# A PEER encoder kernel: VectorE's work beside each unit in a new order, two gate buffers, nine weight buffers

## The chip, the cores and the metric

The kernel runs on one core of a Trainium2 chip. The metric is the device time of one execution, in microseconds. A core has TensorE (matmuls, PE in the profile, with PEld for its weight loads), VectorE (DVE), ScalarE (ACT), GpSimd (POOL) and SyncE (SP), each with a queue of its own that is worked off in order; SyncE, ScalarE and GpSimd also issue DMA transfers.

## What is computed

One encoder layer on 512 tokens of width 2048, all in float32: an input projection, attention and a recurrence side by side, an output projection, and then PEER, a mixer that picks for each token and each of 8 heads the best 16 of 16,384 single-neuron experts. The change lies in the PEER part:

```python
def peer(x, w_pq, sub_k1, sub_k2, u_emb, v_emb):
    q = (xt @ w_pq).reshape(T, PEER_HEADS, 2, PEER_HALF)
    s1 = jnp.einsum('thd,hkd->thk', q[:, :, 0], sub_k1, preferred_element_type=jnp.float32)
    s2 = jnp.einsum('thd,hkd->thk', q[:, :, 1], sub_k2, preferred_element_type=jnp.float32)
    ...
    sc, sel = lax.top_k(cand, PEER_TOPK)
    eidx = jnp.take_along_axis(cidx, sel, axis=-1)
    gates = jax.nn.softmax(sc, axis=-1)
    ...
        uc = u_emb[ic]
        act = jax.nn.gelu(jnp.einsum('cd,ced->ce', xc, uc))
        vc = v_emb[ic]
        return jnp.einsum('ce,ced->cd', (gc * act).astype(vc.dtype), vc)
```

## The kernel before

**Two ways to the same sum.** For the first 160 tokens the chosen rows of `u_emb` and `v_emb` are gathered: 160 row steps with U and 160 with V, each one indirect DMA of GpSimd (128 rows of 2048) into one of three `gat` buffers and one VectorE instruction over it (`gu` L1159, `gv` L1181). The generator `gather_gen` does one such step whenever it is advanced. For the other 352 tokens PEER is computed densely: all 16,384 experts, in 128 blocks of 128, with a matrix of gates that is zero for experts not chosen.

**Units.** The dense part is a chain of 256 units of TensorE with 48 matmuls each. A U block (`u_block`) multiplies a block of U with the 352 tokens and gives `ga`, its gelu. A V unit (`v_unit`) multiplies one of eight chunks of V with eight weighed blocks and adds to `acc` (`v_evict`, two VectorE additions). Every matmul is done three times on values that are split in a high and a low part, so each unit first needs its operand split: a 1 MB load `raw` (SyncE, two buffers), `hi`, a cast on ScalarE (L280), and `lo`, a subtraction on VectorE (L292), two buffers each. `take` at the start of a unit issues the split of the next unit. The low part of a unit is needed by its second or third matmul.

**Stages of the dense part.** The number of U blocks ahead of the first V unit is `lead0`, 31. The first 28 of them carry hooks, four in each block, one after every fourth of its matmuls. `stage_plan` fills the hooks with what is left of the routing (`pair`, `sc`, `pick`, softmax) and then with 88 steps (`g`) that build the gate matrix: VectorE makes two one-hots of 128x512 for a group of four tokens (L1219), ScalarE multiplies one of them by the gates in four instructions (L1222), four TensorE matmuls give the gates, ScalarE copies them out (`stg`, L1227), and after every eight steps a store puts 2 MB in DRAM (`gd`). The plan also sets the steps of the gather (`tick`). It counts costs for TensorE, VectorE and ScalarE and adds a task when VectorE and ScalarE stand no later than TensorE. The first 14 hooked blocks are called routing below, the other 14 the one-hot stage.

Then come 16 passes of eight V units each; between two passes stand the U blocks that are still missing: three in each of the first four passes (short passes), up to eight later (long passes). Before a pass, its eight blocks must be weighed (`weigh`): VectorE multiplies `ga` by the gates in `G` (L1333), ScalarE casts the product (`Wh`, L1336), VectorE subtracts (`Wl`, L1337). `G` holds four blocks, has one buffer and is loaded anew by SyncE after the fourth of them is weighed. There are ten buffers of `Wh` and `Wl` (PR + LEAD). A block whose weighing comes long after its U block is stored to DRAM and reloaded into `gr` (two buffers); these are 38.

**What sets the order.** The order on each engine is that of the program text; no scheduler changes it. In a V unit VectorE gets: lo of the next unit, the eviction of this unit, in two units of a pass a weighing, then the due row steps (1.3 a unit). In a U block: lo of the next, the due row steps, then the weighings that `W_AT` (long passes) or a rule of three per block (short passes) puts there.

## Time and profile before

| | |
|---|---|
| three runs | 3173.66, 3175.65, 3178.24 us, median 3175.65 |
| the profiled execution | 3176.04 us; span 3174.2 |
| mean granted clock of TensorE | 0.972 |
| busy: PE, DVE, ACT, POOL | 93%, 71%, 38%, 26% of the span |
| the dense part | from 878.9 us to the end |

The span reaches from the first to the last instruction; the time has some 2 us around it. A granted clock of 1.00 is TensorE's full 2.4 GHz, and the other level is 1.2 GHz. Busy shares are means over stages that differ, so the table of stages below is read first, and then the waits of each stage: who stood still, and what ended it.

### The profile page before, as it was taken

The page shows a single profiled execution, that of the slowest core. Times are in us where ns is not written, and L with a number is a line of the kernel's source. Part 1 is how long each engine was busy: PE and PEld are TensorE (multiplying, and loading weights), DVE is VectorE, ACT ScalarE, POOL GpSimd, SP SyncE. Part 2 cuts the span into 40 slices and gives each one's busy share as a digit, 9 for nine tenths or more (in the row PEclk, how much of TensorE's full clock was granted, in tenths as well). Part 3 has the DMA queues.
Part 4 walks back from the last instruction along what each step waited for, and adds up shares of the span by engine and source line. Part 5 has one row for each costly group of instructions (what it writes and reads, how often), then busy time and mean ns, then how long its engine had stood idle before and what let it go on. Part 6 is the DMA issues. An engine that isn't in the chain of part 4 may idle for free. (4 is left out here: it accounts for less than half of the span.)

```text
span 3174.2 us, 41739 instructions
## 1 busy us (share of the span) xinstructions
PE 2967.4 (93%) x16965; PEld 2751.6 (87%) x16965; DVE 2251.3 (71%) x3099; ACT 1199.9 (38%) x1705; POOL 823.8 (26%) x539
## 2 busy tenths in 40 slices
PE   8999999999997888689888999999999999999998
PEld 6777766788887888689788999999999999999997
DVE  5763466447975888457767787877777778777875
ACT  5652344334443777232222233233232232232323
POOL 0000211023532113123322323332323323323321
PEclk9999999999998999889899999999999999999999
DMA  5212311242235778778777889889888899898883
GB/s 219 86 69 97 127 47 40 80 160 83 80 136 205 276 285 302 256 275 314 257 288 279 320 312 336 319 318 334 319 322 335 311 335 331 308 337 323 314 307 141
DMA packets 155728, 760.64 MB, mean 240 GB/s; under 512 B 13200, under 2 KB 68000, under 8 KB 69584
## 3 DMA queue, kind: packets, MB, share of 16 engines
q1 hardware_dynamic: 99264, 375.38, 32.8%
q0 software_dynamic: 48000, 345.73, 29.0%
q10 hardware_dynamic: 8272, 36.87, 3.0%
q8 instruction: 133, 2.18, 0.3%
q14 instruction: 59, 0.48, 0.0%
HBM read 719.36 MB, written 38.57 MB: 239 GB/s over the span
## 5 line engine op out<-in xcount | busy, mean ns | idle before, releaser
L292 DVE TENSOR_TENSOR lo<-raw,hi 128x2048 fp32r<-128x2048 f32 x307 | 707.9, 2307 | 404.7 <-ACT hi L280 400.9
L280 ACT CAST hi<-raw 128x2048 fp32r<-128x2048 f32 x316 | 602.2, 1906 | 632.7 <-PE ps_v L1370 276.8
L308 PE MATMUL ps_u<-H,hi 128*128 128x352 f32 x2048 | 674.2, 329 | 37.2 <-ACT hi L280 37.2
L310 PE MATMUL ps_u<-H,lo 128*128 128x352 f32 x2048 | 671.6, 328 | 29.9 <-DVE lo L292 29.7
L1369 PE MATMUL ps_v<-Wh,hi 128*128 128x352 f32 x2048 | 663.4, 324 | 33.1 <-ACT hi L280 27.2
L1371 PE MATMUL ps_v<-Wh,lo 128*128 128x352 f32 x2048 | 667.4, 326 | 16.2 <-DVE lo L292 16.2
L309 PE MATMUL ps_u<-L,hi 128*128 128x352 f32 x2048 | 668.9, 327 | 0.0
L1370 PE MATMUL ps_v<-Wl,hi 128*128 128x352 f32 x2048 | 665.1, 325 | 0.5
L1173 POOL DMA_INDIRECT gv<-in_v_emb_dram,idx x160 | 305.0, 1906 | 735.5 <-DVE gu L1159 550.2
L1157 POOL DMA_INDIRECT gu<-in_u_emb_dram,idx x160 | 299.7, 1873 | 737.4 <-DVE x L1181 542.2
L308 PEld LDWEIGHTS ps_u<-H,hi 128*128 128x128 f32 x2048 | 392.4, 192 | 39.1 <-ACT hi L280 38.9
L310 PEld LDWEIGHTS ps_u<-H,lo 128*128 128x128 f32 x2048 | 391.6, 191 | 36.5 <-DVE lo L292 36.5
L1369 PEld LDWEIGHTS ps_v<-Wh,hi 128*128 128x128 f32 x2048 | 388.3, 190 | 37.6 <-ACT hi L280 30.3
L1371 PEld LDWEIGHTS ps_v<-Wh,lo 128*128 128x128 f32 x2048 | 388.1, 190 | 21.8 <-DVE lo L292 21.7
L309 PEld LDWEIGHTS ps_u<-L,hi 128*128 128x128 f32 x2048 | 392.2, 192 | 0.0
L1370 PEld LDWEIGHTS ps_v<-Wl,hi 128*128 128x128 f32 x2048 | 387.6, 189 | 2.0 <-DVE Wl L1337 2.0
L1159 DVE SCALAR_TENSOR_TENSOR gu<-gu,xng 128x2048 f32<-128x2048 f32 x160 | 365.1, 2284 | 19.3 <-DMA gu<-in_u_emb_dram,idx 19.3
L1181 DVE SCALAR_TENSOR_TENSOR x<-gv,w,x 128x2048 f32<-128x2048 f32 x128 | 300.2, 2345 | 0.1
L1381 DVE TENSOR_TENSOR acc<-ps_v,acc 128x352 f32<-128x352 f32 x240 | 123.8, 521 | 160.1 <-PE ps_v L1371 159.3
L1131 ACT ACTIVATE ga<-ps_u 128x352 f32<-128x352 f32 x128 | 59.0, 461 | 385.9 <-PE ps_u L310 385.9
L1222 ACT ACTIVATE ohA<-ohA,lt 128x128 f32<-128x128 f32 x352 | 112.6, 392 | 56.6 <-DVE ohA L1219 53.7
L1336 ACT CAST Wh<-ga 128x352 fp32r<-128x352 f32 x90 | 43.7, 485 | 237.4 <-DVE ga L1333 237.4
(310 smaller groups left out, 3781.9 us busy)
## 6 DMA issues: line engine op xcount, KB each, us to landing
raw<-in_u_t_dram SPq DMA_DIRECT2D x128, 1024.0 KB
raw<-in_v_t_dram SPq DMA_DIRECT2D x128, 1024.0 KB
raw<-in_w_dram SPq DMA_DIRECT2D x28, 1024.0 KB
gd<-stg ACTq DMA_DIRECT2D x11, 2048.0 KB
G<-gd SPq DMA_DIRECT2D x32, 704.0 KB
raw<-in_w_out_dram SPq DMA_DIRECT2D x16, 1024.0 KB
raw<-in_w_pq_dram SPq DMA_DIRECT2D x16, 1024.0 KB
ad<-ga ACTq DMA_DIRECT2D x38, 176.0 KB
```

What stands on the lines that cost most here:

```text
L280: A.copy(hi, raw)
L292: en.tensor_tensor(lo[:, c], raw[:, c], hi.bitcast(F32)[:, c], op=ALU.subtract)
L308: T.matmul(ps, ah, bh, start=first, stop=False)
L309: T.matmul(ps, ah, bl, start=False, stop=False)
L310: T.matmul(ps, al, bh, start=False, stop=last)
L1157: P.indirect_dma_start(out=g, out_offset=None, in_=u_emb, in_offset=bass.IndirectOffsetOnAxis(ap=ix, axis=0))
L1159: V.scalar_tensor_tensor(out=g, in0=g, scalar=1.0, in1=xs_t["x"], op0=ALU.mult, op1=ALU.mult, accum_out=a_t[h][:, k:k + 1])
L1173: P.indirect_dma_start(out=g, out_offset=None, in_=v_emb, in_offset=bass.IndirectOffsetOnAxis(ap=ix, axis=0))
L1181: V.scalar_tensor_tensor(out=d, in0=g, scalar=wk, in1=d, op0=ALU.mult, op1=ALU.add)
L1369: T.matmul(ps[:, 0:TD], hi[:, cc], Wh, start=j == 0, stop=False)
L1370: T.matmul(ps[:, 0:TD], hi[:, cc], Wl, start=False, stop=False)
L1371: T.matmul(ps[:, 0:TD], lo[:, cc], Wh, start=False, stop=j == PR - 1)
```

## The change

*Planner.* `LEAD` falls from 2 to 1, so there are nine weight buffers. The costs of the planner's tasks are raised, VectorE starts with 4 us on its account, and an engine that is early is credited with 2 us instead of 4. `lead0` becomes 40: 37 U blocks carry hooks, with the same 88 gating steps (one to three in a hook) and 33 row steps, and 55 blocks are stored and reloaded instead of 38. There are six short passes with three U blocks (two in the weighing order 3, 2, 2), one with seven, and then eight and seven. In the long passes one block is weighed beside each U block.

*Gating.* For steps with even number VectorE multiplies the one-hot by the gates in one instruction of 128x512, in place of ScalarE's four.

*Gather.* The rows are issued two steps ahead of the step that uses them, and a task `prime` issues the first two some time before the first step.

*Beside a unit.* A new function, `beside`, is called at the start of each unit after `take`: at most one due row step, then lo of the next unit, then the eviction of the V unit before (it was done in that unit itself), then the weighings, and then a second row step if it is due. `flush_lo` is also called ahead of each hook.

*Buffers.* `G` has two buffers and is loaded two groups ahead; `gr` has three, `ua` three instead of four. The scratch `jk` moves to PSUM.

*Last pass.* The pieces of the final output follow V units 5, 6 and 7 instead of 4, 5 and 6, and the last block is weighed after the last U block.

```diff
-LEAD = 2
+LEAD = 1
-W_AT = ((), (0,), (1,), (), (2, 3), (4,), (5,), ())
...
-        dve, act = max(dve, pe - 4), max(act, pe - 4)
+        dve, act = max(dve, pe - 2), max(act, pe - 2)
...
         for i in range(r):
...
+            ready = [b for b in todo if b < done + i]
+            now = ready[:-(-len(todo) // (r - i))]
+            todo = todo[len(now):]
             run.append(now)
+            order += [("w", b) for b in now] + [("u", done + i)]
...
-        elif b < seen[-1] - 3:
+        elif b < seen[-1] - 1:
             spilled.add(b)
...
-    uap, _ = pool("ua", bufs=4, side="right")
+    uap, _ = pool("ua", bufs=3, side="right")
...
         load_x(0)
...
+        tiles = [issue(*f) for f in seq[:2]]
+        yield
+        for n, (kind, h, k) in enumerate(seq):
+            if n + 2 < len(seq):
+                tiles.append(issue(*seq[n + 2]))
+            (u_step if kind == "u" else v_step)(tiles.pop(0), h, k)
...
-        for t in range(NB):
-            A.activation(out=Ao[:, t, :], in_=Ao[:, t, :], func=AF.Copy, scale=lt[:, 2, ta + t:ta + t + 1])
+        if n % 2:
+            for t in range(NB):
+                A.activation(out=Ao[:, t, :], in_=Ao[:, t, :], func=AF.Copy, scale=lt[:, 2, ta + t:ta + t + 1])
+        else:
+            V.tensor_tensor(Ao, Ao, lt[:, 2, ta:ta + NB].unsqueeze(2).to_broadcast([128, NB, 128]), op=ALU.mult)
...
-    gp, _ = pool("G", bufs=1)
-    sml, _ = pool("sml", bufs=2)
-    grp, _ = pool("gr", bufs=2)
+    gp, _ = pool("G", bufs=2)
+    grp, _ = pool("gr", bufs=3)
...
-            load_g(b // GRP + 1)
+            load_g(b // GRP + 2)
...
-    def tick():
-        due["now"] += due["per"]
+    late_ev = []
+
+    def beside(ws=(), gather=True):
+
+        if gather:
+            due["now"] += due["per"]
+        if due["now"] >= 1.0:
+            due["now"] -= 1.0
+            next(gg, None)
+        flush_lo()
+        while late_ev:
+            v_evict(*late_ev.pop(0))
+        for b in ws:
+            weigh(b)
         while due["now"] >= 1.0:
             due["now"] -= 1.0
             next(gg, None)
...
-                jk = sml.tile([128, 512], F32, tag="jk", name="jk", bufs=1)
+                jk = psB.tile([128, 512], F32, tag="B", name="jk")
...
-            pss = v_unit(g, c)
-            v_evict(g, c, pss)
+            pss = v_unit(g, c, (b0,) if c == 1 and 0 < g < NP - 1 else (), g < NP - 1)
+            late_ev.append((g, c, pss))
...
-                if c in (4, 5, 6):
-                    final(c - 4)
+                if c in (5, 6, 7):
+                    final(c - 5)
...
         for ws in runs[g]:
-            u_block(ub)
+            u_block(ub, beside=lambda: beside(ws))
             ub += 1
-            tick()
-            for b in ws:
-                weigh(b)
```

The order of VectorE in a short pass, beside two of its U blocks, before (`gu` and `x<-gv` are row steps, `gr<-gr,G` and `Wl` a weighing):

```order
L292 TENSOR_TENSOR lo_11661<-raw_11542,hi_11660 128x2048
L1159 SCALAR_TENSOR_TENSOR gu_11718,act_10977<-gu_11718,xng_7449 128x2048
L1333 TENSOR_TENSOR gr_11276<-gr_11276,G_11084 128x352
L1337 TENSOR_TENSOR Wl_11723<-gr_11276,Wh_11722 128x352
L1333 TENSOR_TENSOR gr_11344<-gr_11344,G_11084 128x352
L1337 TENSOR_TENSOR Wl_11730<-gr_11344,Wh_11729 128x352
L1333 TENSOR_TENSOR gr_11726<-gr_11726,G_11733 128x352
L1337 TENSOR_TENSOR Wl_11739<-gr_11726,Wh_11738 128x352
L292 TENSOR_TENSOR lo_11745<-raw_11603,hi_11744 128x2048
L1181 SCALAR_TENSOR_TENSOR x2_0_2586<-gv_11802,w_10974,x2_0_2586 128x2048
L1159 SCALAR_TENSOR_TENSOR gu_11805,act_10977<-gu_11805,xng_7449 128x2048
```

and the same place of the changed kernel:

```order
L1154 SCALAR_TENSOR_TENSOR gu_11241,act_11338<-gu_11241,xng_7444 128x2048
L1173 SCALAR_TENSOR_TENSOR x2_0_2586<-gv_11305,w_11244,x2_0_2586 128x2048
L281 TENSOR_TENSOR lo_11393<-raw_11248,hi_11392 128x2048
L1321 TENSOR_TENSOR gr_11318<-gr_11318,G_10741 128x352
L1325 TENSOR_TENSOR Wl_11403<-gr_11318,Wh_11402 128x352
L1321 TENSOR_TENSOR gr_11325<-gr_11325,G_10741 128x352
L1325 TENSOR_TENSOR Wl_11410<-gr_11325,Wh_11409 128x352
L1154 SCALAR_TENSOR_TENSOR gu_11336,act_11338<-gu_11336,xng_7444 128x2048
L281 TENSOR_TENSOR lo_11468<-raw_11309,hi_11467 128x2048
```

Row steps and weighings still follow lo, but a due row step now stands ahead of each lo, and two weighings stand beside the later U blocks instead of three.

SyncE's DMA issues from the last hooked blocks into the first pass, before (`G` is a gate tile, `gr` a reloaded block):

```order
L266 DMA raw<-in_u_t_dram 128x2048 x31
L1327 DMA G<-gd 128x11x128
L1322 DMA gr<-ad 128x352 x2
L266 DMA raw<-in_v_t_dram 128x2048 x2
L1322 DMA gr<-ad 128x352 x3
L1327 DMA G<-gd 128x11x128
L1322 DMA gr<-ad 128x352 x2
L266 DMA raw<-in_v_t_dram 128x2048
```

and after:

```order
L255 DMA raw<-in_u_t_dram 128x2048 x40
L1315 DMA G<-gd 128x11x128 x2
L1310 DMA gr<-ad 128x352 x3
L255 DMA raw<-in_v_t_dram 128x2048
L1310 DMA gr<-ad 128x352 x3
L255 DMA raw<-in_v_t_dram 128x2048
L1315 DMA G<-gd 128x11x128
```

Two gate tiles and three blocks are loaded ahead of the first weighing, and the third gate tile is issued after the fourth weighing, as the second was before.

VectorE in the one-hot stage, before: the second half of what stands beside one U block (`ohA`, `ohB` are the one-hots, two for a step; three more steps stand ahead of these rows):

```order
L1159 SCALAR_TENSOR_TENSOR gu_8697,act_7451<-gu_8697,xng_7449 128x2048
L1219 TENSOR_TENSOR ohA_8714<-io_sb_88,lt_7938 128x512
L1219 TENSOR_TENSOR ohB_8713<-io_sb_88,lt_7938 128x512
L1219 TENSOR_TENSOR ohA_8728<-io_sb_88,lt_7938 128x512
L1219 TENSOR_TENSOR ohB_8727<-io_sb_88,lt_7938 128x512
L1219 TENSOR_TENSOR ohA_8742<-io_sb_88,lt_7938 128x512
L1219 TENSOR_TENSOR ohB_8741<-io_sb_88,lt_7938 128x512
L1159 SCALAR_TENSOR_TENSOR gu_8754,act_7451<-gu_8754,xng_7449 128x2048
L292 TENSOR_TENSOR lo_8761<-raw_8466,hi_8760 128x2048
```

and after, all that stands beside one U block (L1214 is the new multiplication):

```order
L281 TENSOR_TENSOR lo_9384<-raw_9162,hi_9383 128x2048
L1208 TENSOR_TENSOR ohA_9416<-io_sb_88,lt_8021 128x512
L1208 TENSOR_TENSOR ohB_9415<-io_sb_88,lt_8021 128x512
L1208 TENSOR_TENSOR ohA_9430<-io_sb_88,lt_8021 128x512
L1208 TENSOR_TENSOR ohB_9429<-io_sb_88,lt_8021 128x512
L1214 TENSOR_TENSOR ohA_9430<-ohA_9430,lt_8021 128x512
L1208 TENSOR_TENSOR ohA_9453<-io_sb_88,lt_8021 128x512
L1208 TENSOR_TENSOR ohB_9452<-io_sb_88,lt_8021 128x512
L1154 SCALAR_TENSOR_TENSOR gu_9314,act_9128<-gu_9314,xng_7444 128x2048
L1208 TENSOR_TENSOR ohA_9484<-io_sb_88,lt_8021 128x512
L1208 TENSOR_TENSOR ohB_9483<-io_sb_88,lt_8021 128x512
L1214 TENSOR_TENSOR ohA_9484<-ohA_9484,lt_8021 128x512
```

Four steps and one row step stand between two lo there, where six steps and two row steps stood; two of the four steps have the multiplication on VectorE.

## Rows read from the trace of the kernel before

**Rows 1.** Busy time by stage (stretch and its length in us, then busy time and instructions of PE, PEld, DVE, ACT and POOL, the granted clock of TensorE, the busy share of the DMA engines, GB/s): routing, one-hot stage, opening of the passes, short passes, long passes, last pass, tail.
```profile
878.90:1030.00 151.10, 124.61 (x732) 121.89 (x731) 100.85 (x318) 62.84 (x79) 43.21 (x48) 0.92 0.47 170
1030.00:1267.70 237.70, 202.55 (x1381) 193.28 (x1380) 199.35 (x235) 177.48 (x460) 49.76 (x29) 0.98 0.78 287
1267.70:1339.80 72.10, 46.35 (x242) 43.72 (x242) 34.85 (x34) 17.88 (x24) 8.82 (x7) 0.81 0.69 240
1339.80:1798.90 459.10, 403.74 (x2403) 397.70 (x2402) 316.67 (x275) 119.66 (x110) 133.09 (x65) 0.93 0.78 287
1798.90:3033.40 1234.50, 1226.01 (x7634) 1220.75 (x7633) 972.33 (x793) 368.93 (x326) 393.16 (x207) 1.00 0.88 325
3033.40:3157.60 124.20, 119.34 (x719) 113.63 (x718) 79.76 (x70) 43.49 (x62) 23.87 (x17) 0.99 0.59 216
3157.60:3174.20 16.60, 1.48 (x12) 0.99 (x10) 6.94 (x13) 6.39 (x12) 3.71 (x3) 0.62 0.48 174
```

**Rows 2.** Waits of TensorE in the short passes, 1339.8 to 1798.9 (who waited for whom: us in total, times, longest).
```profile
PE ps_u L308 <- ACT hi L280: 33.4, 4, 9.2
PE ps_v L1369 <- ACT hi L280: 9.1, 3, 6.2
PE ps_v L1371 <- DVE lo L292: 7.3, 6, 1.7
```

**Rows 3.** The same in the long passes, 1798.9 to 3033.4.
```profile
PE ps_v L1371 <- DVE lo L292: 5.8, 8, 1.2
PE ps_u L310 <- DVE lo L292: 2.3, 5, 0.7
```

**Rows 4.** Waits of VectorE in the routing stage, 878.9 to 1030.
```profile
DVE gu L1159 <- DMA gu<-in_u_emb_dram,idx: 19.3, 2, 10.1
```

**Rows 5.** Waits of TensorE in the routing stage.
```profile
PE ps_u L310 <- DVE lo L292: 19.5, 6, 5.8
```

**Rows 6.** Waits of VectorE in the one-hot stage, 1030 to 1267.7.
```profile
DVE lo L292 <- ACT hi L280: 35.3, 14, 4.3
```

**Rows 7.** VectorE in order of time in the one-hot stage, from the last row step of one U block into the next block (start, us, instruction, tiles; in brackets the idle time before it and what ended it).
```profile
1113.17 2.29 DVE L1159 SCALAR_TENSOR_TENSOR gu<-gu,xng 128x2048 f32<-128x2048 f32 x1
...
1117.54 2.29 DVE L292 TENSOR_TENSOR lo<-raw,hi 128x2048 fp32r<-128x2048 f32 x1 [2.08 <-ACT hi L280]
1119.75 0.68 DVE L1219 TENSOR_TENSOR ohA<-io_sb,lt 128x512 f32<-128x512 f32 x1
1120.35 0.68 DVE L1219 TENSOR_TENSOR ohB<-io_sb,lt 128x512 f32<-128x512 f32 x1
```

**Rows 8.** ScalarE over the same moment.
```profile
1113.58 1.29 ACT L1222 ACTIVATE ohA<-ohA,lt 128x128 f32<-128x128 f32 x4
1114.76 0.46 ACT L1131 ACTIVATE ga<-ps_u 128x352 f32<-128x352 f32 x1
...
1115.61 1.90 ACT L280 CAST hi<-raw 128x2048 fp32r<-128x2048 f32 x1 [0.40 <-ACT ga L1131]
```

**Rows 9.** TensorE over the same moment: the one-hot matmuls of three steps (24 records) between two U blocks.
```profile
1116.31 2.90 PE L1242 MATMUL ps_G<-ohA,ohB 128*128 128x128 f32 x24
1118.96 0.41 PE L308 MATMUL ps_u<-H,hi 128*128 128x352 f32 x1
```

**Rows 10.** SyncE's DMA issues in the opening of the passes.
```profile
1280.32 0.61 SPq L1327 DMA_DIRECT2D G<-gd  x1
...
1282.93 1.13 SPq L266 DMA_DIRECT2D raw<-in_v_t_dram  x2
```

**Rows 11.** VectorE in the opening of the passes: the first weighing.
```profile
1287.80 0.53 DVE L1333 TENSOR_TENSOR gr<-gr,G 128x352 f32<-128x352 f32 x1 [4.82 <-DMA gr<-ad]
```

**Rows 12.** Waits of VectorE in the short passes.
```profile
DVE gr L1333 <- DMA G<-gd: 32.8, 4, 9.1
...
DVE gr L1333 <- DMA gr<-ad: 12.2, 3, 5.5
```

**Rows 13.** VectorE in a short pass: three weighings beside one U block.
```profile
1397.19 0.52 DVE L1333 TENSOR_TENSOR gr<-gr,G 128x352 f32<-128x352 f32 x1
...
1398.70 0.52 DVE L1333 TENSOR_TENSOR gr<-gr,G 128x352 f32<-128x352 f32 x1
...
1406.52 0.53 DVE L1333 TENSOR_TENSOR gr<-gr,G 128x352 f32<-128x352 f32 x1 [6.22 <-DMA G<-gd]
```

**Rows 14.** TensorE behind it: the first matmul of the U block that follows.
```profile
1409.42 0.66 PE L308 MATMUL ps_u<-H,hi 128*128 128x352 f32 x1 [8.01 <-ACT hi L280]
```

**Rows 15.** VectorE's groups in the long passes (line, engine, operation, tiles, shapes, count, busy us, mean ns, idle before).
```profile
L292 DVE TENSOR_TENSOR lo<-raw,hi 128x2048 fp32r<-128x2048 f32 x159 | 364.1, 2290 | 103.6 <-ACT hi L280 99.8 <-issue 3.8
L1159 DVE SCALAR_TENSOR_TENSOR gu<-gu,xng 128x2048 f32<-128x2048 f32 x100 | 228.1, 2284 | 0.0
L1181 DVE SCALAR_TENSOR_TENSOR x<-gv,w,x 128x2048 f32<-128x2048 f32 x84 | 197.0, 2345 | 0.1
L1381 DVE TENSOR_TENSOR acc<-ps_v,acc 128x352 f32<-128x352 f32 x161 | 83.2, 521 | 97.6 <-PE ps_v L1371 96.9
```

**Rows 16.** GpSimd's gather issues in the one-hot stage.
```profile
1134.22 0.94 POOL L1157 DMA_INDIRECT gu<-in_u_emb_dram,idx  x1 [4.72 <-DVE x L1181]
```

**Rows 17.** GpSimd's gather issues in the long passes.
```profile
2494.29 2.75 POOL L1157 DMA_INDIRECT gu<-in_u_emb_dram,idx  x1 [6.49 <-DVE x L1181]
```

**Rows 18.** GpSimd in the last pass and the tail: its costliest group.
```profile
L1434 POOL TENSOR_TENSOR o<-o,gf 128x512 f32<-128x512 f32 (+1 forms) x12 | 15.1, 1284 | 40.7 <-ACT jk L1433 40.7
```

More of the change, by code (lines that the diff above doesn't have):

```diff
@@ L109, in stage_plan @@
             dve, act, pe = dve + cost[0], act + cost[1], pe + cost[2]
-            if t[0] == "soft_b" and t[1] == 0:
-                ticks_on = True
+            if t[0] == "prime":
+                ticks_on, since = True, -9.0
             if ticks_on:
@@ L121, in stage_plan @@
     done, runs, order = lead0, [], [("u", b) for b in range(lead0)]
-    for b in range(PR + LEAD):
-        order.append(("w", b))
+    order += [("w", b) for b in range(PR + LEAD)]
     for g in range(NP - 1):
         b0 = (g + 1) * PR
-        r = min(max(3, b0 + PR + LEAD - done), NBLK - done)
-        if g == NP - 2:
-            r = NBLK - done
-        todo = list(range(b0 + LEAD, b0 + PR))
-        run = []
+        r = NBLK - done if g == NP - 2 else min(max(3, b0 + PR + LEAD - done), NBLK - done)
+        todo, run = list(range(b0 + LEAD, b0 + PR)), []
         if g:
-            order += [("w", b0), ("w", b0 + 1)]
+            order.append(("w", b0))
         for i in range(r):
-            order.append(("u", done + i))
-            if r >= 7:
-                k = sum(len(W_AT[j]) for j in range(i + 1))
-                now = [b for b in todo if b < b0 + LEAD + k and b < done + i]
-            else:
-                now = [b for b in todo if b < b0 + LEAD + 3 * (i + 1) and b < done + i]
-            if i == r - 1:
-                now = list(todo)
-            for b in now:
-                todo.remove(b)
-                order.append(("w", b))
+            ready = [b for b in todo if b < done + i]
+            now = ready[:-(-len(todo) // (r - i))]
+            todo = todo[len(now):]
             run.append(now)
+            order += [("w", b) for b in now] + [("u", done + i)]
+        assert not todo or todo == [NBLK - 1]
+        order += [("w", b) for b in todo]
         done += r
@@ L1120, in tile_encoder, with u_block @@
     acts = {}
-    def u_block(b, hook=None):
+    def u_block(b, hook=None, beside=None):
         hi, lo = take()
+        if beside:
+            beside()
         ps = psB.tile([128, 512], F32, tag="B", name="ps_u")
@@ L1167, in act_step, with v_step @@
             w_t[h] = w
-        def v_step(h, k):
-            s = h * TOPK + k
-            ix = idx[:, s:s + 1] if h < NH else idx1[:, s - NSLOT:s - NSLOT + 1]
-            g = gat.tile([128, D], F32, tag="gat", name="gv")
-            P.indirect_dma_start(out=g, out_offset=None, in_=v_emb,
-                                 in_offset=bass.IndirectOffsetOnAxis(ap=ix, axis=0))
+        def v_step(g, h, k):
             wk = w_t[h][:, k:k + 1]
@@ L1286, in tile_encoder @@
           "soft_b": soft_b, "free": lambda _: free_rt(), "g": g_step, "tick": lambda _: step(),
-          "rep": lambda _: rep_lists(), "pre": g_onehots, "lists": lambda t: lts.update({t: g_lists(t)})}
-    st["defer"] = False
+          "prime": lambda _: next(gg), "rep": lambda _: rep_lists(), "pre": g_onehots, "lists": lambda t: lts.update({t: g_lists(t)})}
     flush_lo()
-    load(st["split"])
-    load(st["split"] + 1)
     psS[:] = [psA, "A"]
@@ L1352, in tile_encoder, with v_unit @@
     load_g(0)
-    reload()
-    reload()
-    for i, n in enumerate((0, 5, PR + LEAD)):
-        u_block(lead0 - 3 + i)
-        tick()
-        for b in range((0, 0, 5)[i], n):
-            weigh(b)
-    def v_unit(g, c):
+    load_g(1)
+    for _ in range(3):
+        reload()
+    for i in range(3):
+        u_block(lead0 - 3 + i, beside=lambda: beside(range((0, 3, 6)[i], (3, 6, PR + LEAD)[i])))
+    def v_unit(g, c, ws, gather=True):
         hi, lo = take()
+        beside(ws, gather)
         pss = []
@@ L1483, in tile_encoder @@
         pass
+    v_evict(*late_ev.pop(0))
     final(3)
```

74 lines of the change are left out of this document (33 added, 41 removed).

## The prediction

> **What bounds the kernel now.** I read the table of stages first [rows 1]. A unit (one U block or one chunk of V) is 48 matmuls of 352 columns, and 256 of them follow one another from 878.9 us on. The long passes give a unit's own length: 1234.5 us less 8.1 us of named waits [rows 1, 3] over 159 units is 7.71 us, and I take 7.68 for the unit with no wait, since a few small pauses are in it. There TensorE is busy 99% of the time at a granted clock of 1.00, so it sets the time and little is left to win. The stages ahead of it are another matter. Against 7.68 us a unit, the excess is 43.6 us in routing (151.1 for 14 units), 130.2 in the one-hot stage (237.7 for 14), 33.7 at the opening of the passes (72.1 for 5), 75.1 in the short passes (459.1 for 50) and 16.7 in the last stretch (124.2 for 14 units). In all of them no single engine is busy all the time: the engines wait for one another in turn. So I read the waits stage by stage.
>
> In routing, VectorE stands 19.3 us for the first two gathered rows, whose transfer was issued only at the step that uses them, and TensorE waits 19.5 us for lo splits that stand behind that [rows 4, 5]. In the one-hot stage VectorE is busy 199.35 of 237.7 us and waits 35.3 us, 14 times, once in each block, for ScalarE's hi [rows 1, 6]. Why can be seen over one block boundary: after the last one-hots ScalarE still does four scalings, the gelu, a pause and hi, until 1117.5, while VectorE has only one row step, until 1115.4 [rows 7, 8]. In the opening and the short passes VectorE stops in the middle of a run of weighings, for the next gate tile or a reloaded block [rows 11 to 13]. ScalarE's cast for that weighing stands ahead of the next hi, and so TensorE loses 8.01 us at the next block [rows 14]; four such waits sum to 33.4 us [rows 2]. The granted clock of these stages, 0.81 and 0.93 against 1.00 in the long passes [rows 1], is part of the same loss: after such a stop some matmuls run at 1.2 GHz.
>
> **The change, part by part.** The sum is made against the profiled execution, 3176.0 us for a span of 3174.2; the median of the runs is 3175.65, so the two agree. Stages are compared at equal content: a U block that moves ahead of the passes takes 7.68 us along.
>
> *Routing, 16 blocks instead of 14.* The generator is primed nine VectorE-microseconds ahead of the first step, so the 19.3 us of waiting should go. The rest of the excess is queued top-16 work ahead of lo; the new plan again puts a "sc" and a "pair" in neighbouring hooks, so I leave it. Gain 19; between 0 (the wait covered other lateness) and 34 (all waits and the slow clock, 0.92, go).
>
> *One-hot stage, 21 blocks instead of 14.* Before, a block has 88/14 = 6.3 steps. VectorE's work starts every 0.60 us for a one-hot, 1.21 a step, with lo at 2.21 and a row step at 2.3 [rows 7]: 6.3 x 1.21 + 2.21 + 29/14 x 2.3 = 14.6, and with 2.5 of waiting (35.3/14) 17.1, against 16.98 measured. So VectorE is the bound there, wait included. TensorE alone would need 7.68 + 6.3 x 0.88 = 13.2 (24 records of three steps in 2.65 us [rows 9]). After, a block has 4.19 steps, and half of them have one operation more on VectorE, which I price as a one-hot of the same 128x512, 0.60: 4.19 x 1.51 + 2.21 + 29/21 x 2.3 = 11.7, and TensorE 7.68 + 4.19 x 0.88 = 11.4. What decides is the wait for hi. Where the last step's scaling is now on VectorE, ScalarE's 1.29 us [rows 8] go and VectorE's 0.60 come, so 2.1 becomes 0.2; where it isn't, 2.1 stays. The mean is 1.1, a block 12.8, the stage 269 us against 237.7 + 7 x 7.68 = 291.5: gain 22. Bounds: the whole 2.5 stays (298, a loss of 6), or none (11.7, 246, gain 46). ScalarE gets lighter by 44 x 4 scalings and isn't the bound.
>
> *Opening.* The first gate load is issued at 1280.3, 12.6 us after the stage ends, since it waits for the last gd store; the first weighing starts at 1287.8, 20.1 after [rows 10, 11]. This stays, and now two gate loads and three reloads stand ahead of raw on SyncE's queue: I add 3 us (a gate tile of 128x1408 fp32, 0.72 MB, at the stage's 240 GB/s). The first three weighings still block ScalarE's hi for the third block, which so begins some 32 us after the stage's end instead of 15. But the three runs of three weighings are no longer cut by reloads (three buffers for two) and gate loads. I work the five units out to 60 us instead of 72: gain 12, between 0 and 25.
>
> *Short passes, six instead of four.* Four of them lose 75.1 us now, 18.8 each. With two gate tiles the load is issued a half pass ahead; three reload buffers cover the run of three. What is late next is VectorE itself: beside three U blocks it has 3 lo (6.6), 3 x 1.36 row steps (9.3; 287 over 211 units), 7 weighings of 1.51 each [rows 13] (10.6) and one eviction (1.0 [rows 15]), 27.5 us for 23.0 of TensorE. The overflow of 4.5 is met by slack, since lo is needed only at the next unit's start: 7.68 - 2.3 - 2.21 = 3.2 us. I take 2.5 a pass with lumps of two row steps, 15 in all: gain 60. Bounds: nothing lost (75), or overflow twice over, 9 a pass (21). In the eight V units of a pass the load is 2.21 + 3.1 + 1.0 = 6.3 of 7.68, so the lag is made good.
>
> *Long passes.* lo now stands ahead of the eviction and the weighing, so most of the 8.1 us of waits [rows 3] and the pauses with them go: of 1234.5 - 159 x 7.68 = 13.4, I take 10; between 0 and 13. The deferred eviction costs nothing while psA has four banks and the next unit but one needs them. The gather issue two ahead changes little: with three buffers GpSimd waits for the same VectorE step either way.
>
> *Last pass.* Fewer weighings are left for the last block (gain some 8), but the third final piece comes after the last V unit, and GpSimd's three products of 1.28 us each [rows 18] go into the tail: 4 lost. Net gain 4; between -5 and 10. Scratch in PSUM in place of SBUF: nothing.
>
> Sum: 19 + 22 + 12 + 60 + 10 + 4 = 127, and 3176 - 127 = **3049 us**. All upper bounds together give 2973, all lower ones 3166.
>
> **The rivals.** *VectorE stays the bound in both crowded stages*: the hi wait stays 2.5 us a block (-6), and each short pass loses 9 (21). 19 - 6 + 12 + 21 + 10 + 4 = 61, so 3115. For it: its demand is 11.7 us against TensorE's 11.4 in a one-hot block, and 27.5 against 23.0 in the U blocks of a short pass. Against: it waits, not works, for 35.3 and 45.0 us there now [rows 6, 12].
>
> *The second gate tile doesn't load ahead*, since SyncE issues in order and stands behind a reload's wait. Then six short passes lose 18.8 each, 113 instead of 75, and the sum is 19 + 22 + 12 - 38 + 10 + 4 = 29: 3147. Against: in the order of instructions each gate load stands a group of four blocks earlier, and the reloads ahead of it wait for weighings that are done.
>
> *Slower: gathered rows land late.* Each unit now begins on VectorE with a row step and lo behind it. A row that lands d us late delays lo by d, and past 3.2 us of slack TensorE stands, 211 times. From 127/211 = 0.6 us a unit on, the kernel is slower than before; rows 4 us late would lose 0.8 a unit, 169 in all, and give 3218. For it: the short passes will ask for more than the DMA engines moved in any stage: a raw tile and a row are 128x2048 fp32, 1.05 MB, so a pass of 11 units takes 11.5 MB of raw, 15.7 of rows and 3.4 of gates, reloads and spills, some 31 MB in 85 us or 360 GB/s, against 325 at a share of 0.88 [rows 1]. Against: in the long passes, with the same three buffers and 1.3 rows a unit, row steps find their row (0.0 and 0.1 us of idle time [rows 15]). A gather's issue takes 0.94 us in the one-hot stage and 2.75 in the long passes [rows 16, 17], with VectorE busier in the first (84% against 79%), so VectorE's work isn't what stretches it. The Trainium skill (SBUF — State Buffer, "Who interferes with whom") has a rule that would feed this rival: a VectorE instruction with two SBUF inputs blocks a GpSimd instruction that reads SBUF, and this change gives VectorE 44 more of those. By that rule the one-hot stage, full of them, should have the longest issues; the trace shows the shortest, so I don't raise the chance; if the rule held here, the time would be this rival's 3218 and not 3049.
>
> **How the numbers follow.** Forecast (gains of 80 to 171): 0.70. VectorE bound: 0.13. No load ahead: 0.04. Late rows: 0.06. Better than 3005: 0.07. The range reaches from 3005, with the forecast's lower side, to 3112, which takes in the nearer half of the VectorE rival; about 0.8 lies inside. A measurement of this kernel can tell 0.2%, 6 us, from no change. Faster by more: 0.92; within: 0.02; slower: 0.06.
>
> **What would show it.** Right: the one-hot stage ends near 1295 us and the first V unit begins near 1338, with 37 and 40 U blocks behind them instead of 28 and 31; no wait for G in the short passes, and 87 us a pass; short passes at a clock near 1.00; VectorE's share over 90% in them; row waits near zero. Wrong: lo waits for hi of 2 us or more in each one-hot block; TensorE's waits for lo of over 3 us in each short pass; VectorE waiting for gathered rows; raw landing late behind the gate loads; a tail over 21 us.

## The result

The changed kernel takes 3061.93 us (median of 4 runs, 3060.12 to 3072.61) against 3174.65 us before (4 runs, 3170.77 to 3178.24): a ratio of 0.9652, 95% interval 0.9627 to 0.9677. The prediction was 3049 us, 13 us too low and within its range. The profiled execution took 3060.12 us, with a span of 3058.3.

Busy time by stage in the profile after, columns as in [rows 1]: routing, one-hot stage, opening, short passes, long passes, last pass, tail.

```profile
878.50:1020.60 142.10, 132.69 (x828) 130.76 (x827) 101.89 (x312) 64.96 (x73) 53.58 (x46) 0.99 0.50 182
1020.60:1293.50 272.90, 247.46 (x1716) 241.30 (x1716) 247.44 (x294) 146.38 (x306) 82.04 (x30) 1.00 0.76 283
1293.50:1357.70 64.20, 44.32 (x243) 42.76 (x242) 34.53 (x33) 17.24 (x22) 14.88 (x7) 0.81 0.86 311
1357.70:1872.80 515.10, 500.81 (x3074) 495.85 (x3074) 415.40 (x367) 155.47 (x143) 169.41 (x86) 0.99 0.92 343
1872.80:2919.60 1046.80, 1046.28 (x6530) 1045.76 (x6530) 852.42 (x695) 315.96 (x273) 331.86 (x187) 1.00 0.90 336
2919.60:3036.90 117.30, 114.99 (x707) 111.02 (x707) 72.03 (x65) 41.61 (x58) 18.75 (x13) 1.00 0.57 207
3036.90:3058.30 21.40, 4.23 (x25) 2.62 (x23) 8.40 (x17) 8.34 (x18) 7.48 (x6) 0.62 0.37 135
```

The stages hold other numbers of units now (16, 21, 5, 64, 136 and 14), so I compare what each loses, its length less 7.68 us a unit:

| stage | lost before | lost after | gain | predicted |
|---|---|---|---|---|
| routing | 43.6 | 19.2 | 24.4 | 19 |
| one-hot | 130.2 | 111.7 | 18.5 | 22 |
| opening | 33.8 | 25.7 | 8.1 | 12 |
| short passes | 75.0 | 23.6 | 51.4 | 60 |
| long passes | 13.4 | 2.3 | 11.1 | 10 |
| last pass and tail (its whole length) | 33.4 | 31.2 | 2.2 | 4 |
| sum | | | 115.7 | 127 |

The gains sum to the difference of the two spans, 115.9 us. The losses are worked out from unit starts before rounding, so a stage may differ by 0.2 from its row.

Waits of VectorE, then of TensorE, in the short passes after (who waited for whom, us in total, times, longest). The gate rows, 32.8 us in four waits before [rows 12], don't appear; reloads do, five times in six passes. TensorE's 33.4 us for hi [rows 2] are gone; the largest of what it still waits for, 6.2 us in all, is the weights (Wh) of V units.

```profile
DVE lo L281 <- ACT hi L269: 60.3, 28, 5.1
DVE Wl L1325 <- ACT Wh L1324: 24.9, 45, 0.6
DVE gr L1321 <- DMA gr<-ad: 10.9, 5, 4.1
```
```profile
PE ps_v L1368 <- ACT Wh L1324: 6.2, 5, 3.4
PE ps_v L1370 <- DVE lo L281: 3.8, 2, 1.9
PE ps_u L299 <- DVE lo L281: 3.6, 5, 1.3
```

One of the waits for a reload in order of time, SyncE's DMA issues and then VectorE: the reload that the pass's last weighing uses is the first of the two issued from 1421.31 on, when the third weighing before it had freed a buffer; the weighing stands 2.28 us until it lands.

```profile
1421.31 1.83 SPq L1310 DMA_DIRECT2D gr<-ad  x2
1427.26 0.33 SPq L255 DMA_DIRECT2D raw<-in_v_t_dram  x1
1428.78 0.32 SPq L1310 DMA_DIRECT2D gr<-ad  x1
```
```profile
1427.15 0.52 DVE L1321 TENSOR_TENSOR gr<-gr,G 128x352 f32<-128x352 f32 x1
...
1431.03 0.53 DVE L1321 TENSOR_TENSOR gr<-gr,G 128x352 f32<-128x352 f32 x1 [2.28 <-DMA gr<-ad]
```

SyncE's gate issues in the opening after, which answer to [rows 10]:

```profile
1308.99 1.49 SPq L1315 DMA_DIRECT2D G<-gd  x2
```

Three more waits after: VectorE's in the one-hot stage, 1.1 us a block where [rows 6] had 2.5; TensorE's longest in the opening, the third U block; and all that is left of TensorE's in the long passes, where [rows 3] had 8.1 us.

```profile
DVE lo L281 <- ACT hi L269: 24.0, 13, 3.4
```
```profile
PE ps_u L297 <- ACT hi L269: 14.9, 1, 14.9
```
```profile
PE ps_v L1368 <- DVE acc L1380: 0.5, 2, 0.3
```

### The profile page after: what moved, and what is told of

The parts are those of the page before. It is cut to its first block, busy times and chain, and to the rows that moved or that the text cites. A ratio compares the mean times of both kernels' runs of the same rounds, so it can differ in the third digit from the quotient of the medians.

```text
span 3058.3 us, 41550 instructions
## 1 busy us (share of the span) xinstructions
PE 2933.6 (96%) x16965; PEld 2729.7 (89%) x16965; DVE 2272.5 (74%) x3143; ACT 1153.3 (38%) x1529; POOL 846.3 (28%) x539
## 3 DMA queue, kind: packets, MB, share of 16 engines
q1 hardware_dynamic: 101712, 378.44, 33.8%
## 5 line engine op out<-in xcount | busy, mean ns | idle before, releaser
L297 PE MATMUL ps_u<-H,hi 128*128 128x352 f32 x2048 | 666.8, 326 | 14.9 <-ACT hi L269 14.9
L299 PE MATMUL ps_u<-H,lo 128*128 128x352 f32 x2048 | 662.5, 323 | 14.3 <-DVE lo L281 14.3
L298 PE MATMUL ps_u<-L,hi 128*128 128x352 f32 x2048 | 661.3, 323 | 0.0
L1147 POOL DMA_INDIRECT gu<-in_u_emb_dram,idx x160 | 331.6, 2073 | 691.4 <-DVE x L1173 500.9
L1147 POOL DMA_INDIRECT gv<-in_v_emb_dram,idx x160 | 286.7, 1792 | 658.8 <-DVE gu L1154 466.1
L297 PEld LDWEIGHTS ps_u<-H,hi 128*128 128x128 f32 x2048 | 385.9, 188 | 15.4 <-ACT hi L269 15.2
L1368 PEld LDWEIGHTS ps_v<-Wh,hi 128*128 128x128 f32 x2048 | 386.7, 189 | 10.8 <-ACT Wh L1324 8.0
L298 PEld LDWEIGHTS ps_u<-L,hi 128*128 128x128 f32 x2048 | 385.9, 188 | 0.0
L1324 ACT CAST Wh<-ga 128x352 fp32r<-128x352 f32 x73 | 35.5, 487 | 223.3 <-DVE ga L1321 223.3
L297 PE MATMUL ps_cm<-xh,hi 128*128 128x512 f32 x256 | 106.0, 414 | 11.5 <-ACT xh L369 9.1
L1234 PE MATMUL ps_G<-ohA,ohB 128*128 128x128 f32 x704 | 92.0, 279 | 25.4 <-ACT stg L1219 17.4
## 6 DMA issues: line engine op xcount, KB each, us to landing
gd<-stg ACTq DMA_DIRECT2D x11, 2048.0 KB, 10.1
```

The lines of the kernel that those rows point to most:

```text
L297: T.matmul(ps, ah, bh, start=first, stop=False)
L298: T.matmul(ps, ah, bl, start=False, stop=False)
L299: T.matmul(ps, al, bh, start=False, stop=last)
L1147: P.indirect_dma_start(out=g, out_offset=None, in_=u_emb if kind == "u" else v_emb, in_offset=bass.IndirectOffsetOnAxis(ap=ix, axis=0))
L1234: T.matmul(ps[:, t, :], B[:, t, :], Ao[:, t, :], start=True, stop=True)
L1368: T.matmul(ps[:, 0:TD], hi[:, cc], Wh, start=j == 0, stop=False)
```

## The experiments

All but the last are single runs, against the changed kernel's profiled execution (3060.12 us) unless another is named. Whole times of one kernel spread: five runs of the last one lie between 3045.0 and 3056.4. Stages repeat better where an edit doesn't touch them: the one-hot stage takes 273.0 us in nine of these runs, the short passes 512.8 to 518.3 in five executions, the long passes 1046.0 to 1047.4 in seven, routing 141.5 to 143.7. So I read each run by what its stages lose. "Loses 21.3 us for 2.3" gives this run's loss first and then that of the kernel it is compared with.

### What the second gate buffer is worth

`one_gate`:

```diff
-    gp, _ = pool("G", bufs=2)
+    gp, _ = pool("G", bufs=1)
...
-            load_g(b // GRP + 2)
+            load_g(b // GRP + 1)
...
     load_g(0)
-    load_g(1)
```

> The changed kernel with one gate buffer, each gate load issued when the weighing before it has been issued, as in the kernel before; four of the units' other edits stay. Theory (the second gate tile is the largest single part of the gain): VectorE waits for the gate rows again, 8.2 us in each pass of three weighings as in the kernel before, of which the new order hides little; short passes +35 to +55 us, opening +3 to +8, long passes 0 to +10; whole time 3100 to 3130 us. Rival (the order of VectorE's work alone, evictions ahead of the wait, hides the wait): short passes 0 to +10, whole time 3060 to 3072 us.

3103.17 us, 43 more, as the theory said, but not where it said. The short passes lose 23.7 us, as with two buffers (23.6). The 43 us lie in the opening (39.6 for 25.7), the long passes (21.3 for 2.3), the last pass (14.6 for 9.8) and some 5 us ahead of the one-hot stage, which the edit doesn't touch. VectorE's waits for the gate rows, in the opening and in the long passes (none in the short passes):

```profile
DVE gr L1321 <- DMA G<-gd: 17.3, 2, 8.7
```
```profile
DVE ga L1321 <- DMA G<-gd: 37.4, 9, 7.8
```

So with one buffer, for which VectorE waited 8.2 us a pass before, the new short pass never waits for the gate rows. VectorE there, in order of time: a gate group of four ends with the last weighing of one U block (1430.17), SyncE issues the next group's load at 1430.71, and the next weighing comes beside the next U block, at 1438.36, with nothing to wait for.

```profile
1430.17 0.52 DVE L1321 TENSOR_TENSOR gr<-gr,G 128x352 f32<-128x352 f32 x1
...
1438.36 0.52 DVE L1321 TENSOR_TENSOR gr<-gr,G 128x352 f32<-128x352 f32 x1
```

In the long passes one block is weighed beside a unit, so that a gate group ends between two units there as well. Yet VectorE waits nine times, because the load takes longer than a unit. At the longest wait the next group's load is issued at 2100.70, and the first weighing that needs it starts 14.5 us later; above, 7.7 us were enough. Why these loads take longer isn't shown.

```profile
2100.70 0.53 SPq L1315 DMA_DIRECT2D G<-gd  x1
```
```profile
2115.17 0.53 DVE L1321 TENSOR_TENSOR ga<-ga,G 128x352 f32<-128x352 f32 x1 [7.82 <-DMA G<-gd]
```

New theory: what counts in a short pass is whether a gate group ends between two U blocks or in the middle of one block's run of weighings. Before, it ended in the middle [rows 13]. Three runs test that.

`before_222`, the kernel before with one number changed:

```diff
-                now = [b for b in todo if b < b0 + LEAD + 3 * (i + 1) and b < done + i]
+                now = [b for b in todo if b < b0 + LEAD + 2 * (i + 1) and b < done + i]
```

> The kernel before with one number changed: a short pass weighs two, two and two blocks beside its three U blocks, where it weighed three, three and none, so that the fourth block of a gate group is a U block's last weighing and the next group's first comes a U block later. All else, the one gate buffer, the order and the planner, stays as before. Theory (in the short passes it was the place of the weighings against the gate groups that made VectorE wait for the gate rows, and one gate buffer does there): four waits of 8.2 us go and the pile of three weighings with them; the short passes, which lose 75 us beyond 7.68 us a unit, lose 25 to 45; whole time 3128 to 3150 us. Rival (the gate rows late behind the pass's other transfers need the second gate tile): short passes 0 to 10 us shorter, whole time 3165 to 3178 us.

3140.38 us against 3173.23 us (median of 9 runs of the kernel before). The short passes lose 39.2 us where they lost 75.0: 35.8 us from one number, with one gate buffer and the old order. The row of the short passes, VectorE's wait for the gate rows and TensorE's for hi at a U block (32.8 and 33.4 us before):

```profile
1336.40:1759.60 423.20, 401.82 (x2402) 394.81 (x2401) 317.99 (x276) 120.00 (x109) 130.35 (x66) 0.96 0.85 314
```
```profile
DVE gr L1333 <- DMA G<-gd: 7.7, 3, 3.6
```
```profile
PE ps_u L308 <- ACT hi L280: 0.2, 1, 0.2
```

`g1_232`, one gate buffer (the edit of `one_gate`) and, in the planner:

```diff
-            now = ready[:-(-len(todo) // (r - i))]
+            now = ready[:(2, 3, 2)[i] if r == 3 else -(-len(todo) // (r - i))]
```

> The changed kernel with one gate buffer, as in the run with one gate buffer, and with two, three and two weighings beside a short pass's three U blocks where the change has three, two and two, so that a gate group ends in the middle of one U block's three weighings. Theory (the place of the weighings against the gate groups decides in the short passes): six waits of about 8 us for the gate rows come back, the short passes lose 50 to 75 us in place of 23.7; whole time 3130 to 3155 us. Rival (one U block's turn is enough for any order): within 6 us of the run with one gate buffer, 3097 to 3109 us.

3156.44 us, 53 more than `one_gate`. The short passes lose 75.6 us for 23.7. The waits are back, one in each pass, on VectorE and then on TensorE (five of the six; the last falls on the border to the long passes):

```profile
DVE gr L1321 <- DMA G<-gd: 61.3, 6, 11.1
```
```profile
PE ps_v L1367 <- ACT hi L269: 43.2, 5, 9.3
```

The long passes, which the edit leaves alone, lose 31.4 for 21.3 in `one_gate`. Of the 10.1 us more, 5.1 lie in their first unit, right behind the sixth of these waits, and belong to it; the rest stays open.

`g2_232`, the same line with two gate buffers:

> The changed kernel with its two gate buffers and with two, three and two weighings beside a short pass's three U blocks where the change has three, two and two. Theory (with two gate buffers the place of the weighings against the gate groups decides nothing): the short passes within 8 us of the changed kernel's, whole time 3054 to 3070 us. Rival (it is not the gate rows but the three weighings in the pass's middle that cost): short passes 25 us or more longer, whole time 3085 us or more.

3076.99 us, with the short passes losing 34.4 us for 23.6 and the long ones 7.4 for 2.3. That lies between theory and rival. The gate rows don't appear, as the theory said, but the place of the weighings still costs 10.8 us, and VectorE's waits for reloads grew from 10.9 to 22.2 us:

```profile
DVE gr L1321 <- DMA gr<-ad: 22.2, 5, 6.3
```

The place of the weighings is thus worth 51.9 us in the short passes with one gate buffer and 10.8 with two, and the second buffer 41.2 with the bad place and 0.1 with the good one. In the short passes either alone does most of it.

### The last reload of a short pass

`gr4` (two small tiles move to another pool to make room):

```diff
-    grp, _ = pool("gr", bufs=3)
+    grp, _ = pool("gr", bufs=4)
...
-    for _ in range(3):
+    for _ in range(4):
         reload()
```

> The changed kernel with four buffers for the accumulator reloads in place of three, and four reloads issued at the start. Theory (the 3.9 us lost in each short pass are mostly the last weighing's wait for its reload, which is issued only after a weighing has freed a buffer): short passes 8 to 11 us shorter, what they lose beyond 7.68 us a unit falling from 23.6 to 12 to 16 us; whole time 3049 to 3054 us. Rival (VectorE's work of a short pass, 27.5 us beside 23.0 in a unit's turn, is what is lost): short passes 0 to 3 us shorter, whole time 3058 to 3062 us.

3050.67 us. The short passes lose 11.1 us for 23.6: 12.5 us less, a little more than expected. No wait for a reload is left, nor TensorE's for Wh. The row of the short passes:

```profile
1360.30:1862.90 502.60, 495.58 (x3074) 492.70 (x3073) 415.15 (x367) 155.66 (x143) 171.72 (x86) 1.00 0.94 351
```

VectorE does the same work as in the changed kernel (415.15 and 415.40 us), so the 12.5 us were no overflow of its work. TensorE's busy time falls by 5.2 us as well (500.81 to 495.58), at a granted clock of 1.00 for 0.99. The 11.1 us that are left may be overflow in part: TensorE's wait for lo at a U block is 3.6 us in five times here too.

### Ahead of the passes: planner, gating, rows

`plan_old`, the planner's old costs (two of the eight changes shown):

```diff
-        tasks += [("pair", 6.9, 0.0, 0.0)]
+        tasks += [("pair", 6.2, 0.0, 0.0)]
...
-    pe, dve, act = 0.0, 4.0, 0.0
+    pe, dve, act = 0.0, 0.0, 0.0
```

> The changed kernel with the planner's old costs of the U, V and gating work, so that the routing and gating steps stand where the kernel before had them; the split of the gating, the rows two ahead, the order, the gate buffers and the weight buffers are as changed. Theory (the split of the gating needs the planner that spreads it, and the blocks drawn into the gating stage shorten the short passes): opening with 4 units fewer ahead of it, loss of routing and one-hot stage together 15 to 30 us more than the changed kernel's 130.9, whole time 3075 to 3095 us. Rival (the planner's numbers don't matter, the edits beside them do): 3058 to 3068 us.

3068.04 us, 8 more: between the two. Its stages, counted as before (14, 14, 5 and 50 units up to the long passes):

```profile
877.00:1013.00 136.00, 122.60 (x739) 120.91 (x738) 102.09 (x316) 61.45 (x73) 49.32 (x47) 0.95 0.50 181
1013.00:1253.40 240.40, 201.47 (x1373) 193.90 (x1372) 225.89 (x280) 129.09 (x288) 78.64 (x29) 0.96 0.75 281
1253.40:1314.90 61.50, 42.37 (x242) 40.81 (x241) 32.28 (x32) 17.24 (x22) 13.89 (x6) 0.83 0.85 304
1314.90:1704.00 389.10, 386.60 (x2403) 384.93 (x2402) 318.61 (x277) 120.56 (x111) 126.10 (x66) 1.00 0.93 349
```

Routing loses 28.5 us and the one-hot stage 132.9, together 30.5 more than with the new costs (130.9), just over the theory's 15 to 30. Most of it comes back: the four short passes lose 5.0 us in all, where the changed kernel's six lose 23.6, and the opening 23.1 for 25.7. The new costs move nine U blocks ahead of the passes and so make two more short passes, the kind with late reloads. That isn't all of it: each of the four loses 1.3 us, each of the six 3.9, and why isn't shown.

`gate_act`, all gating on ScalarE:

```diff
-        if n % 2:
+        if True:
             for t in range(NB):
```

> The changed kernel with all of the one-hot tiles' gating on ScalarE, as in the kernel before; the planner still believes that every second row is VectorE's. Theory (in the gating stage VectorE bounds a block, and each row moved off it saves some 0.5 us of VectorE per unit, while ScalarE has the room): one-hot stage 8 us shorter to 5 us longer, whole time 3052 to 3066 us, so that half the gating on VectorE is worth about nothing. Rival (ScalarE's longer chain delays staging and the hi part, which VectorE's lo part waits for): one-hot stage 12 to 25 us longer, whole time 3072 to 3086 us.

3073.32 us, within the rival's range; by the stages it is less. The one-hot stage is 7.3 us longer (280.3 for 273.0); the rest lies in stages that the edit doesn't touch. VectorE's wait for hi goes from 24.0 us to 2.8 us in each of 21 blocks:

```profile
DVE lo L281 <- ACT hi L269: 58.5, 21, 4.3
```

So VectorE is freed of work but then waits for ScalarE; the split is worth some 7 us.

`no_ahead`, each gathered row issued at its own step:

```diff
-        tiles = [issue(*f) for f in seq[:2]]
+        tiles = []
...
-            if n + 2 < len(seq):
-                tiles.append(issue(*seq[n + 2]))
+            tiles.append(issue(*seq[n]))
```

> The changed kernel with each gathered row issued at the step that uses it, none two steps ahead; the start of the routing stage then waits for its first rows as the kernel before did (two waits of 9.7 us). Theory (the early issue of the first rows is a good part of the routing stage's gain of 24 us): routing stage 10 to 19 us longer, one-hot stage unchanged within 4 us, whole time 3070 to 3082 us. Rival A (the planner's costs did it, the waits for the rows were covered): 3058 to 3066 us. Rival B (every step then waits for its row): 10 us or more for each of the 11 rows, 3150 us or more.

3060.18 us, no change: rival A. Routing loses 20.7 us for 19.2, but it also loses 20.7 or 20.8 in five runs whose edit doesn't touch it (`one_gate`, `g2_232`, `gr4`, `opening`, `best`), so the edit costs nothing that can be seen. VectorE does wait again, once and not twice as expected; TensorE's wait for lo is 9.4 us in five waits in both kernels, so that wait was hidden.

```profile
DVE gu L1154 <- DMA gu<-in_u_emb_dram,idx: 7.4, 1, 7.4
```
```profile
PE ps_u L299 <- DVE lo L281: 9.4, 5, 3.4
```

### Order, opening, final pieces

`lo_last`:

```diff
-        flush_lo()
         while late_ev:
             v_evict(*late_ev.pop(0))
         for b in ws:
             weigh(b)
+        flush_lo()
```

> The changed kernel with VectorE's work beside a unit back in the old order: eviction and weighing of the block before come first, then the new block's lo part. Theory (lo first is what ended the long passes' wait for lo): long passes 6 to 10 us longer for the 17 blocks of evictions, short passes 5 to 20 us longer as the weighings stand ahead of lo, whole time 3072 to 3092 us. Rival (with the gate rows early no wait is left that the order decides): within 3 us of the changed kernel, 3058 to 3065 us.

3065.47 us, a size that a single run can't tell from none. By stages the long passes lose 4.8 us for 2.3 and the short ones 22.6 for 23.6. Nearly the rival: the order is worth 2.5 of the long passes' 11.1 us. The edit is no full return to the old order, though: the row step ahead of a unit's work and the one weighing a unit stay. TensorE's waits for lo in the long passes come to 2.2 us, where [rows 3] had 8.1:

```profile
PE ps_u L299 <- DVE lo L281: 1.7, 4, 0.7
PE ps_v L1370 <- DVE lo L281: 0.5, 1, 0.5
```

`opening`, the first weighings one U block later:

```diff
-        u_block(lead0 - 3 + i, beside=lambda: beside(range((0, 3, 6)[i], (3, 6, PR + LEAD)[i])))
+        u_block(lead0 - 3 + i, beside=lambda: beside(range((0, 0, 4)[i], (0, 4, PR + LEAD)[i])))
```

> The changed kernel with the first block's weighings one U block later (none in the first of the three, four in the second, five in the third, where the change has three, three and three). Theory (the first weighing waits on its reload, which stands behind two gate loads, and holds the hi part's way through ScalarE and VectorE): what the opening loses beyond 7.68 us a unit falls from 25.7 to 12 to 17 us; whole time 3046 to 3053 us. Rival (the raw rows and weights come late in any order, because the two gate loads and the reloads share the transfers with them): opening 0 to 3 us shorter, whole time 3057 to 3062 us.

3062.16 us; the opening loses 25.8 us for 25.7. TensorE's wait for hi only moves, from the third U block (14.9 us) to the first V unit, so the theory falls. What sets the opening's length beyond the late gate store and loads isn't separated.

```profile
PE ps_v L1368 <- ACT hi L269: 12.3, 1, 12.3
```

`pieces`:

```diff
-                if c in (5, 6, 7):
-                    final(c - 5)
+                if c in (4, 5, 6):
+                    final(c - 4)
```

> The changed kernel with the three final pieces at the fourth, fifth and sixth unit of the last pass's end, as in the kernel before, in place of one unit later. Theory (the tail's 4.7 us more than before are GpSimd's products of a piece that comes too late): tail 4 to 5 us shorter, last pass 0 to 2 us longer, whole time 3056 to 3059 us. Rival (the pieces then wait in the middle of the last pass and hold TensorE there): tail shorter by 4 to 5 and last pass longer by as much, whole time 3060 to 3063 us.

3056.36 us. The tail is 4.2 us shorter and the last pass 3.2 longer, net 1.0: the rival, nearly. The rest of the 3.8 us lies in stages that the edit doesn't touch. Last pass and tail:

```profile
2916.80:3037.40 120.60, 116.61 (x720) 112.36 (x719) 74.46 (x69) 43.63 (x64) 22.54 (x16) 1.00 0.56 201
3037.40:3054.60 17.20, 1.73 (x12) 1.01 (x10) 6.29 (x13) 6.28 (x12) 3.71 (x3) 0.66 0.46 168
```

### Two edits together

`best` is the changed kernel with the edits of `gr4` and `pieces`.

> The changed kernel with four buffers for the accumulator reloads and the final pieces one unit earlier, the two edits that shortened it when made alone. They lie in different stages (short passes; last pass and tail), so that their gains should add: 9.4 and 3.8 us off the changed kernel's time, 3046 to 3051 us. Rival (single looks that differ by 3 us by themselves): 3052 to 3060 us.

3052.31 us (median of 5 runs, 3045.0 to 3056.4), a ratio to the kernel before of 0.9611, 95% interval 0.9589 to 0.9632, where the changed kernel has 0.9652 (0.9627 to 0.9677). The median lies in the rival's range, just above the sum. The short passes lose 15.4 us (11.1 in `gr4`, the same code there), last pass and tail together 30.5 for 31.2: the gain is the fourth reload buffer's. The two intervals overlap a little, so a gain of some 9 us on the changed kernel (8.9 by the two stages) is likely, and not more than that.

## Why the prediction came out as it did

The whole was right because its largest terms were right in size. Their causes were less often right, and where a size fits without its cause, as in the long passes, that is luck. In the headings below the first number is the measured gain, the second the predicted one.

**Short passes: 51.4 us for 60.** The step that was mis-sized is "three reload buffers cover the run of three" with "2.5 a pass" for VectorE's overflow: a pass lost 3.9 us. Overflow isn't the whole of it. VectorE is busy 415.40 of 515.1 us there, 81% and not the forecast's over 90%, and a fourth reload buffer takes a third (`best`) to a half (`gr4`) of the loss away with VectorE's work unchanged. So the term put at nothing, the wait for the pass's last reload, cost 8.2 (`best`) to 12.5 us (`gr4`) in the six passes. What is left with the fourth buffer, 1.9 to 2.6 us a pass, is about the 2.5 that I took for overflow, though no run shows that it is overflow. The cause put ahead of it, "with two gate tiles the load is issued a half pass ahead", is true but wasn't needed: `one_gate` loses no more in the short passes, and `before_222` gets 35.8 us without the second tile. I had read the stop at 1406.52 [rows 13] as a load issued too late; the rows show as well that the weighings ahead of it ran on in the same run, so that the load had no unit's time to land in. The edit that I had not priced, three, two and two weighings in place of three, three and none, was enough to end that wait.

**Second rival.** Its price rested on the same step, 18.8 us lost in each short pass if gates aren't loaded ahead. With `one_gate` nothing is loaded ahead, and these passes lose 3.9 each. What one buffer does cost, some 38 of the 43 us, lies in other stages, and the time comes near the rival's 3147 only where the weighings stand badly too: `g1_232`, with both, takes 3156.

**Long passes: 11.1 for 10.** Right size, wrong cause. lo first gives 2.5 us (`lo_last`). With one gate buffer the new order, one weighing a unit, loses 21.3 us, more than the old order's 13.4, which left a unit free at the end of a gate group; here the second buffer is needed. What gave the rest of the gain, the one weighing a unit or the new place of the row steps, was not tried alone.

**Routing: 24.4 for 19.** The cause isn't borne out: the 19.3 us of waiting [rows 4] did go, but under the new plan a wait of 7.4 us comes back at no cost that can be seen (`no_ahead`). The planner's costs are worth 9.3 (28.5 less 19.2). The other 15.1 (43.6 less 28.5) came under the old plan with the rows issued ahead, the order and the flush of lo together; which of them gave it stays open. lo flushed ahead of the hooks' work is what I would try.

**One-hot stage: 18.5 for 22.** Right by its own step: VectorE is busy 11.8 us a block (247.44 over 21) for 11.7, the wait for hi is 24.0 us over 21 blocks, 1.1 each as taken, and a block 13.0 us for 12.8. `gate_act` bears out the reasoning, with 2.8 us of waiting a block. The split gives 7 us; under the old plan it and the other edits together give nothing (132.9 us lost for 130.2 before), so that most of the gain hangs on the costs that spread the steps over 21 blocks.

**Opening: 8.1 for 12; last pass and tail: 2.2 for 4.** The wait for the third block's hi (14.9 us) was named; the gate loads were issued at 1308.99 us, 15.5 after the stage's end, not 12.6. The tail grew by 4.7 us, for the 4 put down for GpSimd's products (GpSimd is busy 7.48 us there, 3.71 before), and moving the piece back takes 4.2 us off it and puts 3.2 on the last pass.

**First and third rival.** The first rival's prices did not come: the wait for hi is 1.1 us a block and not 2.5, and a short pass loses 3.9 and not 9. (Its terms add up to 60, not 61, which gives 3116 us.) But VectorE's work and its wait for hi still fill the one-hot stage, 247.44 and 24.0 of 272.9 us. Rows do not land late: VectorE waits for them 5.5 us in the 136 units of the long passes, at 336 GB/s, and 1.9 us in the short passes at 343, where I had estimated 360. But the argument that I made about the gather's issue was wrong, as the last section shows.

## What to carry to other kernels

Ask where a run of work that shares one loaded tile ends. If it ends between two units, one buffer can be enough, but only where the load lands within a unit: in the short passes it did, in the long passes often not. If it ends inside a unit, the load has no time, and a second buffer hides that at a price in memory. When several edits are made to one wait, take each out alone: two that each remove it look worthless singly, or seem to earn the whole. And a wait in a profile is worth what the bounding engine gets back, not its own length.

## What the runs showed of the hardware that I had not expected

GpSimd's issue of a gather is stretched by VectorE's work after all. [Rows 16] showed one issue of 0.94 us, and I took it for the one-hot stage; it was one made while VectorE waited. The mean there was 2.1 us for u rows, against 1.8 in the long passes, so the one-hot stage did not have the shortest issues. After, the mean there is 3.6 us for u rows. Below are GpSimd's group in that stage, then two of its issues in order of time, one with VectorE mostly idle beside it and one of 9.17 us, and VectorE beside the second: from 1172.76 to 1182.07 it goes without a pause through a lo split, one-hots, a gating and a row step, nearly all of them instructions with two SBUF inputs.

```profile
L1147 POOL DMA_INDIRECT gu<-in_u_emb_dram,idx x20 | 72.0, 3598 | 164.8 <-DVE gu L1154 99.3 <-DVE x L1173 65.6
```
```profile
1132.48 0.94 POOL L1147 DMA_INDIRECT gu<-in_u_emb_dram,idx  x1 [5.88 <-DVE gu L1154]
...
1173.11 9.17 POOL L1147 DMA_INDIRECT gu<-in_u_emb_dram,idx  x1 [5.93 <-DVE x L1173]
```
```profile
1172.76 2.28 DVE L281 TENSOR_TENSOR lo<-raw,hi 128x2048 fp32r<-128x2048 f32 x1
1174.96 0.68 DVE L1208 TENSOR_TENSOR ohA<-io_sb,lt 128x512 f32<-128x512 f32 x1
...
1181.38 0.69 DVE L1208 TENSOR_TENSOR ohA<-io_sb,lt 128x512 f32<-128x512 f32 x1
```

With the gating on ScalarE the mean is 1.8 us (`gate_act`). Of the stage's 30 issues ten took under 1 us. The other 20, from 1.15 to 9.17 us, all end 0.8 us after the end of a VectorE instruction, the one of 9.17 us after the row step that starts at 1179.17 and takes 2.28. A run without a pause is not enough for a long issue: one at 1024.27 has one-hots beside it throughout and took 1.16 us. How many instructions pass before an issue goes on isn't explained. That the long issues end behind a VectorE instruction agrees with the rule of the Trainium skill (SBUF — State Buffer, "Who interferes with whom") that a VectorE instruction with two SBUF inputs contends with a GpSimd instruction that reads SBUF; which resource it is, no run here isolates. The time doesn't suffer, and the rival that I had tied to this rule doesn't follow from it: in that stage VectorE never waits for a row.
